# Convolution steps over GpSimd that begin five column groups later

## The chip, the cores and the metric

The kernel runs on one core of a Trainium2 chip. The metric is the device time of one execution in microseconds, the median of three runs. A core has TensorE (PE; its weight loads are PEld), VectorE (DVE), ScalarE (ACT), GpSimd (POOL) and SyncE (SP), whose queue starts all the transfers here. Each engine works off its own instructions in the order in which they were written, and waits where one needs another engine's result.

## The reference

One inference step of a small diffusion backbone: 2 layers over 1024 sample tokens and 128 prompt tokens of width 1024. In each layer three branches share one input projection, and their outputs go together into one output projection; then comes an MLP.

```python
h = _rms(x, n1) * (1 + sc1) + sh1
u_conv, qa, ka, va, qn, kn, vn = jnp.split(h @ w_in, idx, axis=-1)
a_out = _conv_module(u_conv, dw_w, dw_b, ln_g, ln_b)      # 256 channels, 31 taps over the tokens
...                                                       # b_out: grouped-query attention
...                                                       # c_out: neighbourhood attention
x = x + g1 * (jnp.concatenate([a_out, b_out, c_out], axis=-1) @ w_out)
h = _rms(x, n2) * (1 + sc2) + sh2
x = x + g2 * (jnp.square(jax.nn.relu(h @ w1)) @ w2)

def _conv_module(u, dw_w, dw_b, ln_g, ln_b):
    a, g = jnp.split(u, 2, axis=-1)
    h = a * jax.nn.sigmoid(g)
    h = lax.conv_general_dilated(h, dw_w[:, None, :], ..., feature_group_count=CONV_CH) + dw_b
    return jax.nn.silu(_layer_norm(h, ln_g, ln_b))
```

The convolution is depthwise: each channel is a sum of 31 shifted copies of itself, each times its own weight.

## The kernel before, in words

The program is written out by hand: Python generators are advanced in turn, and what each writes at its turn stands in that place on its engine. Nothing reorders it later.

**Projection** (`project`). The columns of `w_in` come in blocks: V0 and V1 (the convolution's 512 columns), then A0 to A5 and VN, 256 columns each. A0 and A1 hold the queries and keys that get the rotary positions, a good deal of GpSimd work. The seven blocks from A0 on run over five groups of token tiles each, 35 column groups in all, with 48 matmuls for a group of two tiles (tile `pst`). In each group, after the matmuls and ahead of the head norm, `project` advances the convolution by one call. While A5 and VN are written, the start of the attention is already mixed in: key building (tiles `k`, `kd`, `pstr`) and the scan of the first unit's maxima.

**Convolution.** The channels are two halves of 128, j = 0 and j = 1. `cin[j]` is the gated input, `acc[j]` (tile `cacc`) the sum, 1167 elements long. `conv_tap` writes one of the 31 steps. All of half 0, and steps 22 to 30 of half 1, are one VectorE instruction each (L102, `cacc<-cin,vecs,cacc`). Steps 0 to 21 of half 1 go another way: ScalarE makes a scaled copy (tile `cp`, L93) and GpSimd adds it (L596, `cacc<-cacc,cp`); step 0 is ScalarE's alone. `conv_taps` orders them by a counter n, which is 0 in the third of the 35 groups and goes up by one with each call. Half 0 comes first on VectorE. The nine VectorE steps of half 1 may start only when all the 22 others are written, since they add to the same `acc`; then one or two are written in a call, in turn.

After the last step `conv_all` writes the layer norm over both halves in three pieces of the tokens: sums on TensorE (tiles `psmu`, `psvr`), then `cacc<-psmu`, `lsq`, `lrs` and so on on VectorE and ScalarE, one small step to a call, 39 calls. `conv_out` then writes the result into the input of the output projection (tiles `HA`), 16 calls.

**Attention.** `gqa` has six units u = 0 to 5: three pairs of heads, and two halves of the sample tokens. A unit goes over nine key tiles, in two steps each. For each key tile TensorE makes scores (`psst`), ScalarE the exponentials (`pt`), TensorE the weighted sum (`psacc`), and the row sums R are added up: GpSimd for key tiles 1 to 6, VectorE for the last two. In the same steps runs the scan for the next unit: 24 matmuls (`psm`) and 24 maxima over them on VectorE (`mx`), then their spread over TensorE (`nmx`, `psnm`). The eight PSUM banks are shared by all of it. After the scan of unit 0 in the projection's last groups come six units, and `attention` advances the convolution by one call in every second step:

```python
        tail = conv_out(L)
        n = natten(L)
        for i, _ in enumerate(g):
            if i % 2:
                next(tail, None)
            next(fill, None)
            if L.unit == 5 and (not L.prepared or i in (6 * 18 - 5, 6 * 18 - 2)):
                next(n)
        run(tail)
```

The loop has 108 steps, so 54 calls; what is left of the convolution after it is written at once by `run(tail)`. `fill` is the modulation of the layer: a product with the `ada_w` matrix (tiles `aw`, `psmod`, `mt`, `psmt`), at whose end VectorE makes `mod` and `A`. Its weights come through the same SP queue as the projection's weights and the stores of the projected columns. After the units come the neighbourhood attention, the output projection and the MLP, which the change does not touch.

Of the kernel before, what the change touches and what calls it, by code (L numbers as in the profile page):

```python
# [45 lines left out]
def hybrid_step(ctx, tc, I, O, depth=DEPTH):  # L46
# [536 lines left out]
    def conv_tap(L, j, k):  # L583
        cin, acc = L.cin[j], L.acc[j]
        if j == 0 or k >= POOL_TAPS:
            if k == 0:
                ts(acc[:, 0:CW], cin[:, 0:CW], dww(L.l, j, 0), ALU.mult, cvec(L.l, 0, j), ALU.add)
            else:
                stt(acc[:, 0:CW], cin[:, k:k + CW], dww(L.l, j, k), acc[:, 0:CW], ALU.mult, ALU.add)
        else:  # L590
            if k == 0:
                act(acc[:, 0:CW], cin[:, 0:CW], ACTF.Identity, scale=dww(L.l, j, 0), bias=cvec(L.l, 0, j))
            else:
                p = S([CW], n="cp")
                act(p, cin[:, k:k + CW], ACTF.Copy, scale=dww(L.l, j, k))
                nc.gpsimd.tensor_tensor(out=acc[:, 0:CW], in0=acc[:, 0:CW], in1=p, op=ALU.add)  # L596

    def conv_taps(L):

        d = [(0, k) for k in range(CONV_K)] + [(1, k) for k in range(POOL_TAPS, CONV_K)]  # L600
        p = [(1, k) for k in range(POOL_TAPS)]
        n = 0
        while d or p:
            if p and n > 6:
                conv_tap(L, *p.pop(0))
            for _ in range(2 if n <= 6 else 1 + n % 2):
                if d and (d[0][0] == 0 or not p):
                    conv_tap(L, *d.pop(0))
            n += 1
            yield  # L610
# [135 lines left out]

    def conv_all(L):
        yield from conv_taps(L)
        l = L.l
        L.cin = None  # L750
# [1272 lines left out]
```

## Time and profile before

| | |
|---|---|
| median of three runs | 2948.95 us (2948.65 to 2950.8) |
| the profiled execution | 2947.94 us, of it span 2946.1 us |
| TensorE matmul busy | 2835.9 us, 96% of the span |
| VectorE, ScalarE, GpSimd busy | 2036.5, 1419.1 and 651.0 us |
| mean granted TensorE clock | 0.989 |
| projection and grouped-query units of layer 0 | some 120 to 540 us of the span |
| the same of layer 1 | some 1570 to 2000 us |

A row of the chain of waits shows a start, a length and the work that the end of the program depended on at that time. A row of the timeline shows start, length, engine, line, operation, output and input tiles and count, and in brackets how long the engine stood idle before it and what ended that. TensorE's matmuls are pipelined and their ends are modelled, so that a TensorE that is 96% busy may still have waits in it. Times are of the profiled execution, in us from the start of its span.

### The profile page before, as it was taken

Reading aid. Unit: us, or ns where it says so; the run is one execution under the profiler, and the core shown is the slowest. Engines: PE = TensorE matmul, PEld = TensorE weight load, DVE = VectorE, ACT = ScalarE, POOL = GpSimd, SP = SyncE. Lnnn points to the kernel's source line nnn. Section 1 sums busy time; section 2 is a strip of 40 time slices with the busy share of each in tenths; the row PEclk is TensorE's granted clock in tenths of the full one; section 3 lists DMA queues with packets and bytes.
Section 4 is the critical chain, followed back from the end, with each engine's and each line's share of the span. In section 5 each row is a group of like instructions: output and inputs, shape, how many; then the busy total and the mean of one; then the engine's idle time right before and its main releaser. Section 6 shows DMA issues by size and latency. Waiting matters only on the chain.

```text
span 2946.1 us, 52867 instructions
## 1 busy us (share of the span) xinstructions
PE 2835.9 (96%) x20328; PEld 2513.9 (85%) x20328; DVE 2036.5 (69%) x4007; ACT 1419.1 (48%) x2936; POOL 651.0 (22%) x597
## 2 busy tenths in 40 slices
PE   7999999999999999999989999999999999999998
PEld 4789645899999989999878885458999999999998
DVE  6576778855867756668776757778467777585766
ACT  5335366853744443433552454568446444433343
POOL 2577246310000000000236763553100000000000
PEclk9999999999999999999999999999999999999999
DMA  8377202424566678443443780033336665665334
GB/s 291 96 203 203 81 17 56 112 80 133 173 201 207 212 235 297 158 144 96 141 141 86 198 236 27 17 94 78 112 118 205 192 208 190 223 206 183 116 103 161
DMA packets 434876, 444.05 MB, mean 151 GB/s; under 512 B 120512, under 2 KB 308672, under 8 KB 434624
## 3 DMA queue, kind: packets, MB, share of 16 engines
q1 hardware_dynamic: 434624, 440.67, 48.2%
q8 instruction: 160, 2.62, 0.4%
q14 instruction: 92, 0.75, 0.1%
HBM read 307.41 MB, written 133.17 MB: 150 GB/s over the span
## 4 chain that ended last, share of the span: by engine, by line
PE 81%; DVE 8%; DMA 4%; ACT 3%; POOL 2%; issue 2%; SPq 1%; DVEq 0%; POOLq 0%; ACTq 0%
PE ps L1345 23%; PE psb L1345 8%; PE psc L1345 7%; PE pso L1345 5%; PE psa L1345 5%; PE pst L567 3%; PE pst L568 3%; PE pst L569 3%; PE psacc L1144 3%; PE psd L1345 3%; PE pspv L1011 2%; PE pspt L995 2%; PE psst L1158 2%; PE psm L1070 2%; PE psst L1159 1%
## 5 line engine op out<-in xcount | busy, mean ns | idle before, releaser
L1345 PE MATMUL ps<-ts,w2h 128*128 128x288 f32 x3072 | 535.3, 296 | 8.3 <-DVE ts L99 4.8
L1345 PEld LDWEIGHTS ps<-ts,w2h 128*128 128x128 f32 x3072 | 452.4, 189 | 9.2 <-DVE ts L99 5.3
L1345 PE MATMUL ps<-ts,w2l 128*128 128x288 f32 x1536 | 329.0, 295 | 0.0
L96 ACT CAST ts<-ti 128x576 fp32r<-128x576 f32 x256 | 172.1, 672 | 320.8 <-PE ps L1345 147.8
L567 PE MATMUL pst<-wh,HA 128*128 128x256 f32 x1040 | 295.2, 284 | 0.0
L568 PE MATMUL pst<-wl,HA 128*128 128x256 f32 x1040 | 292.0, 281 | 0.0
L569 PE MATMUL pst<-wh,HA 128*128 128x256 f32 x1040 | 291.4, 280 | 0.0
L93 ACT ACTIVATE ev<-ev 128x576 f32<-128x576 f32 x240 | 164.7, 686 | 259.5 <-DVE ev L99 255.7
L1345 PEld LDWEIGHTS ps<-ts,w2l 128*128 128x128 f32 x1536 | 247.6, 189 | 0.2
L102 DVE SCALAR_TENSOR_TENSOR X<-ps,mod,X 128x288 f32<-128x288 f32 x336 | 112.1, 409 | 176.0 <-PE ps L1345 176.0
L99 DVE TENSOR_TENSOR ts<-ti,ts 128x576 fp32r<-128x576 f32 x256 | 199.7, 780 | 32.1 <-ACT ts L96 30.5
L567 PEld LDWEIGHTS pst<-wh,HA 128*128 128x128 f32 x1040 | 195.6, 188 | 19.2 <-PE pst L569 5.2
L568 PEld LDWEIGHTS pst<-wl,HA 128*128 128x128 f32 x1040 | 195.8, 188 | 0.1
L569 PEld LDWEIGHTS pst<-wh,HA 128*128 128x128 f32 x1040 | 195.8, 188 | 0.0
L1813 POOL COPY yu<-X 128x128 f32<-128x128 f32 x8 | 4.0, 510 | 839.4 <-DVE X L102 811.1
L99 POOL TENSOR_TENSOR nacc<-nacc,nsq 128x512 f32<-128x512 f32 x3 | 3.9, 1298 | 791.2 <-PE ps L1345 791.1
L1345 PE MATMUL pso<-HA,woh 128*128 128x288 f32 x1024 | 177.6, 295 | 0.0
L1072 DVE TENSOR_REDUCE mx<-psm 128x1 f32<-128x384 f32 x288 | 142.1, 546 | 29.5 <-PE psm L1070 29.3
L93 ACT ACTIVATE pt<-psst 128x512 f32<-128x512 f32 x216 | 118.0, 597 | 87.1 <-PE psst L1159 86.0
L99 POOL TENSOR_TENSOR R<-R,pt 128x1024 f32<-128x1024 f32 x60 | 149.5, 2492 | 24.5 <-ACT pt L93 22.4
L1345 PEld LDWEIGHTS pso<-HA,woh 128*128 128x128 f32 x1024 | 149.5, 188 | 0.0
L99 DVE TENSOR_TENSOR w1l<-w1r,w1h 128x512 fp32r<-128x512 f32 x128 | 88.0, 689 | 87.0 <-ACT w1h L96 87.0
(281 smaller groups left out, 7229.4 us busy)
## 6 DMA issues: line engine op xcount, KB each, us to landing
ti<-hd SPq DMA_DIRECT2D x128, 576.0 KB, 4.0
hd<-ev SPq DMA_DIRECT2D x224, 288.0 KB, 4.1
w1r<-in_mlp_w SPq DMA_DIRECT2D x176, 256.0 KB, 4.0
aw<-in_ada_w SPq DMA_DIRECT2D x160, 256.0 KB, 4.1
HF<-in_mlp_w SPq DMA_DIRECT2D x128, 256.0 KB, 5.3
ddA<-o SPq DMA_DIRECT2D x144, 128.0 KB, 3.5
wr<-in_w_in SPq DMA_DIRECT2D x28, 512.0 KB, 4.1
sd<-ev SPq DMA_DIRECT2D x24, 576.0 KB, 2.8
```

The source lines that it names most:

```text
L93: nc.scalar.activation(out=out, in_=in_, func=func, scale=scale, bias=bias, **k)
L96: nc.scalar.copy(out, in_)
L99: (eng or nc.vector).tensor_tensor(out=out, in0=a, in1=b, op=op)
L102: nc.vector.scalar_tensor_tensor(out=out, in0=a, scalar=s, in1=b, op0=op0, op1=op1)
L567: mm(o, hi, wh, start=(k == 0), stop=False)
L568: mm(o, hi, wl, start=False, stop=False)
L569: mm(o, lo, wh, start=False, stop=(k == KT - 1))
L995: nc.tensor.transpose(ps[0:n, c], self.p[j][:, o:o + n], ident)
L1011: mm(ps[64 * j:64 * j + 64, 0:128], v[j], self.at[j, i], start=(i == 0), stop=(i == nb - 1))
L1072: nc.vector.tensor_reduce(out=mx[j][:, qt, b:b + 1], in_=ps[:, 0:384], op=ALU.max, axis=AX.X)
L1144: mm(acc[64 * j:64 * j + 64, :], v, pt[:, j, :], start=(kt == 0), stop=(kt == 8))
L1345: mm(ps[h][:, 0:HH], x, y[:, h * HH:(h + 1) * HH], start=(start and z == 0), stop=(stop and z == 2), skip_group_check=True)
```

## The change

One number is other: the counter from which `conv_taps` writes the steps of half 1 that go over GpSimd.

```diff
@@ conv_taps
         p = [(1, k) for k in range(POOL_TAPS)]
         n = 0
         while d or p:
-            if p and n > 6:
+            if p and n > 11:
                 conv_tap(L, *p.pop(0))
             for _ in range(2 if n <= 6 else 1 + n % 2):
                 if d and (d[0][0] == 0 or not p):
                     conv_tap(L, *d.pop(0))
             n += 1
             yield
```

The 22 steps were written in the calls n = 7 to 28, and are now in n = 12 to 33. The nine VectorE steps of half 1 were in n = 28 to 33 (1, 2, 1, 2, 1, 2), and are now in n = 33 to 38 (2, 1, 2, 1, 2, 1). Calls up to n = 32 are made in the projection, VN holding n = 28 to 32; from n = 33 on they are made in the units of the attention, one to a key tile. So all that follows, layer norm and output, moves five calls later too. The steps of half 0 stay. No instruction is added or removed, and both layers get the same order.

VectorE where the VN columns begin, in layer 0. `xn` is the head norm of the last A5 group, `k` and `kp` are the keys of the attention, `q` its queries, `cacc` the convolution. Before, and after:

```order
L99 TENSOR_TENSOR xn_3304<-pst_3262,y_3292 128x128
L99 TENSOR_TENSOR k_3076<-pstr_3256,k_3076 64x128
L99 TENSOR_TENSOR kp_3077<-pstr_3256,kp_3077 64x128
L102 SCALAR_TENSOR_TENSOR cacc_1092<-cin_732,vecs_100,cacc_1092 128x1167
L99 TENSOR_TENSOR k_3326<-pstr_3330,k_3326 64x512
L99 TENSOR_TENSOR k_3326<-pstr_3410,k_3326 64x512
L99 TENSOR_TENSOR k_3326<-pstr_3418,k_3326 64x128
L99 TENSOR_TENSOR kp_3327<-pstr_3418,kp_3327 64x128
L102 SCALAR_TENSOR_TENSOR cacc_1092<-cin_732,vecs_100,cacc_1092 128x1167 x2
L99 TENSOR_TENSOR q_3498<-pstr_3426,q_3431 64x512
```

```order
L99 TENSOR_TENSOR xn_3289<-pst_3247,y_3277 128x128
L99 TENSOR_TENSOR k_3061<-pstr_3241,k_3061 64x128
L99 TENSOR_TENSOR kp_3062<-pstr_3241,kp_3062 64x128
L99 TENSOR_TENSOR k_3311<-pstr_3315,k_3311 64x512
L99 TENSOR_TENSOR k_3311<-pstr_3394,k_3311 64x512
L99 TENSOR_TENSOR k_3311<-pstr_3402,k_3311 64x128
L99 TENSOR_TENSOR kp_3312<-pstr_3402,kp_3312 64x128
L99 TENSOR_TENSOR q_3483<-pstr_3410,q_3415 64x512
```

The steps of half 1 have left VectorE's VN stretch, seven of them in all.

GpSimd at the end of the projection and the begin of unit 0, in layer 0; `o` is the gained head norm that is stored, R the row sums. Before, and after:

```order
L596 TENSOR_TENSOR cacc_1092<-cacc_1092,cp_3298 128x1167
L497 TENSOR_TENSOR o_3287<-xn_3304,gains_527 128x128
L596 TENSOR_TENSOR cacc_1092<-cacc_1092,cp_3388 128x1167
L99 TENSOR_TENSOR R_3756<-pt_3757,pt_3784 128x1024
L99 TENSOR_TENSOR R_3756<-R_3756,pt_3826 128x1024
```

```order
L497 TENSOR_TENSOR o_3272<-xn_3289,gains_527 128x128
L596 TENSOR_TENSOR cacc_1092<-cacc_1092,cp_3373 128x1167
L596 TENSOR_TENSOR cacc_1092<-cacc_1092,cp_3468 128x1167
L596 TENSOR_TENSOR cacc_1092<-cacc_1092,cp_3560 128x1167
L596 TENSOR_TENSOR cacc_1092<-cacc_1092,cp_3645 128x1167
L596 TENSOR_TENSOR cacc_1092<-cacc_1092,cp_3696 128x1167
L596 TENSOR_TENSOR cacc_1092<-cacc_1092,cp_3797 128x1167
L99 TENSOR_TENSOR R_3746<-pt_3747,pt_3774 128x1024
L99 TENSOR_TENSOR R_3746<-R_3746,pt_3819 128x1024
```

Between the last stored head norm and the first R stood one add of the convolution, and now stand six; the last (`cp_3797`) is written in unit 0.

VectorE at the begin of unit 0, in layer 0; `mx` are the maxima of the next unit's scan. Before, and after:

```order
L99 TENSOR_TENSOR q_3793<-pstr_3773,q_3778 64x512
L1072 TENSOR_REDUCE mx_3799<-psm_3801 128x1
L1072 TENSOR_REDUCE mx_3799<-psm_3804 128x1
L102 SCALAR_TENSOR_TENSOR cacc_1092<-cin_732,vecs_100,cacc_1092 128x1167 x2
L99 TENSOR_TENSOR mod_101<-psmt_3809,vecs_100 128x16 x2
L102 SCALAR_TENSOR_TENSOR A_0_103<-mod_101,vecs_100 128x8 x2
L1072 TENSOR_REDUCE mx_3799<-psm_3820 128x1
L1072 TENSOR_REDUCE mx_3799<-psm_3823 128x1
L1072 TENSOR_REDUCE mx_3799<-psm_3835 128x1
L1072 TENSOR_REDUCE mx_3799<-psm_3838 128x1
L1072 TENSOR_REDUCE mx_3799<-psm_3847 128x1
```

```order
L99 TENSOR_TENSOR q_3783<-pstr_3763,q_3768 64x512
L1072 TENSOR_REDUCE mx_3789<-psm_3791 128x1
L1072 TENSOR_REDUCE mx_3789<-psm_3794 128x1
L102 SCALAR_TENSOR_TENSOR cacc_1092<-cin_732,vecs_100,cacc_1092 128x1167 x2
L99 TENSOR_TENSOR mod_101<-psmt_3802,vecs_100 128x16 x2
L102 SCALAR_TENSOR_TENSOR A_0_103<-mod_101,vecs_100 128x8 x2
L1072 TENSOR_REDUCE mx_3789<-psm_3813 128x1
L1072 TENSOR_REDUCE mx_3789<-psm_3816 128x1
L1072 TENSOR_REDUCE mx_3789<-psm_3828 128x1
L1072 TENSOR_REDUCE mx_3789<-psm_3831 128x1
L102 SCALAR_TENSOR_TENSOR cacc_1092<-cin_732,vecs_100,cacc_1092 128x1167
```

Two steps stand at the same place in both, but before they are the last two of half 1 and now the first two; after each four maxima one or two more follow, seven in all, where the layer norm of the first piece stood.

## The prediction

> **What bounds the kernel now.** I read the page's totals first, then a table of windows over the places where the moved instructions stand, then the chain of waits in one of those windows, then the single instructions.
>
> ```profile
> span 2946.1 us, 52867 instructions
> PE 2835.9 (96%) x20328; PEld 2513.9 (85%) x20328; DVE 2036.5 (69%) x4007; ACT 1419.1 (48%) x2936; POOL 651.0 (22%) x597
> ```
>
> TensorE sets the pace over the whole, but the change acts only in two short stages of each of the two layers. In the windows (columns: window, length, then busy time and count for PE, PEld, DVE, ACT, POOL, then granted clock, DMA share, GB/s) layer 0 has the VN columns of the projection, then units 0, 1, 2 and 4 of the grouped-query attention; the last row is unit 0 of layer 1. The borders are mine, a few us wide.
>
> ```profile
> 300.00:320.00 20.00, 20.00 (x163) 19.00 (x161) 16.49 (x23) 2.67 (x6) 1.55 (x1) 1.00 0.43 136
> 326.30:364.00 37.70, 30.89 (x135) 16.63 (x133) 32.70 (x51) 14.15 (x27) 15.69 (x6) 0.98 0.07 20
> 364.00:396.30 32.30, 31.80 (x133) 16.12 (x132) 21.73 (x44) 20.22 (x44) 17.29 (x10) 0.92 0.05 13
> 396.30:429.00 32.70, 29.05 (x126) 14.49 (x124) 27.50 (x43) 19.23 (x34) 15.73 (x7) 1.00 0.09 27
> 459.60:487.00 27.40, 27.12 (x125) 14.30 (x122) 22.81 (x39) 16.33 (x34) 16.18 (x8) 1.00 0.56 144
> 1782.00:1819.00 37.00, 30.32 (x129) 16.30 (x127) 30.97 (x50) 13.41 (x24) 15.77 (x6) 0.95 0.06 17
> ```
>
> In the projection (300 to 320) TensorE is busy all the time and the other engines hide. In the attention units it is not: unit 4 takes 27.4 us, the windows of unit 0 take 37.7 and 37.0 us (the end of the first scan is in them), and VectorE is busy for 32.7 and 31.0 us of them. The chain of waits in unit 0 of layer 0 (start, length, what) says where VectorE is the one waited for:
>
> ```profile
> 329.41 1.03 PE psnm L1061 x8
> ...
> 335.56 2.32 DVE cacc L102
> 337.91 1.43 DVE cacc L102
> 339.34 0.17 DVE mod L99 x2
> 339.51 2.15 DVE A L102 x2
> 341.66 0.48 DVE mx L1072
> ...
> 348.50 2.79 DVE lsq L99
> ...
> 356.27 2.48 DVE lsq L102
> 358.78 0.70 DVE lsq L102
> 359.50 0.69 DVE lrs L102
> 360.19 0.94 DVE mx L1072 x2
> 361.16 0.18 DVE nmx L1055
> 361.38 1.19 PE psnm L1061 x8
> ```
>
> From 335.56 to 342 the chain is convolution work and the modulation vector on VectorE, with the maxima of the next unit (mx) queued behind; TensorE needs those maxima done to get PSUM banks back and to end the unit (psnm). Unit 0 is the stage to price.
>
> **What the change takes out, and its worth.** The 22 steps of channel half 1 that go over GpSimd (one start on ScalarE, then 21 times a scaled copy on ScalarE and an add on GpSimd) keep their number and begin five calls later. Five leave the stretch after the rotary columns. Four enter the VN columns, which had one, and one enters unit 0. The rows of the tiles (ns: least, median, most; first and last start; the third is VectorE's step, called a tap here):
>
> ```profile
> L93 ACT ACTIVATE cp<-cin,vecs x42: 1254/1268/1281, 180.2 to 1752.9; 128x1167 f32<-128x1167 f32 x42
> L596 POOL TENSOR_TENSOR cacc<-cacc,cp x42: 2685/2712/3839, 184.4 to 1754.4; 128x1167 f32<-128x1167 f32 x42
> L102 DVE SCALAR_TENSOR_TENSOR cacc<-cin,vecs,cacc x78: 1417/1436/2727, 127.6 to 1794.7; 128x1167 f32<-128x1167 f32 x78
> ```
>
> Four of each are 10.8 us of GpSimd and 5.1 us of ScalarE. In the first 20 us of VN GpSimd was busy for 1.55 us and ScalarE for 2.67, so this hides. Where they leave, the gain could only come through a store that SP holds for GpSimd, with loads queued behind it. TensorE's waits in the projection of layer 0 are these (all of them from 115 to 326 us, the last of the first kind in order of time, and the next one after 326):
>
> ```profile
> PE psmod L223 <- DMA aw<-in_ada_w: 5.4, 6, 1.5
> PE pstr L810 <- ACT sq L93: 0.5, 1, 0.5
> 181.16 1.67 PE L223 MATMUL psmod<-aw,silc 128*2 128x512 f32 x4 [0.48 <-DMA aw<-in_ada_w]
> 329.41 1.03 PE L1061 MATMUL psnm<-ident,nmx 128*1 128x128 f32 x8 [2.31 <-DVE nmx L1055]
> ```
>
> The first moved add starts at 184.4 us, after the last wait for a load. So the relief is worth 0; at most it is the waits of other kinds, 0.5 and 2.3 us, 2.8 us a layer. DMA traffic is unchanged and the stores stand where they stood.
>
> The nine VectorE steps of half 1 wait for the last GpSimd step. Seven of them stood in VN and two in unit 0; now all nine stand in unit 0, one or two for each of its first six key tiles. What leaves VN frees nothing: TensorE was busy 20.0 of 20.0 us there.
>
> **What the change puts into unit 0.** Four terms, per layer.
>
> (1) The first call. It now issues the last GpSimd step and two VectorE steps that wait for it. The rows of ScalarE and GpSimd at that place:
>
> ```profile
> 333.08 1.12 ACT L93 ACTIVATE pt<-psst 128x512 f32<-128x512 f32 x2
> 334.28 2.35 POOL L99 TENSOR_TENSOR R<-pt,pt 128x1024 f32<-128x1024 f32 x1 [32.72 <-ACT pt L93]
> 338.03 3.52 POOL L99 TENSOR_TENSOR R<-R,pt 128x1024 f32<-128x1024 f32 x1 [1.40 <-ACT pt L93]
> ```
>
> The scaled copy follows the exponentials that end at 334.20 and ends at 335.47; the GpSimd add (2.7 us alone) ends near 338.2. VectorE, free at 335.5, waits 2.7 us, and the maxima behind it wait too. Then comes an exclusion that these rows show: the first tap ran 2.32 us because R held GpSimd until 336.63; R of 338.03 took 3.52 us and not 2.35 because the second tap ran until 339.34; and the two ops on A, of 8 columns, took 2.15 us and ended with that R. A tap that is not hindered takes 1.43. If VectorE goes first at 338.2, its taps end at 341.1, R at 343.45, A at 343.75: 2.1 later than 341.66. If R, queued behind the add, goes first (to 340.55), the taps end at 343.45, the second R then at 345.8, A at 346.05: 4.4 later. Nothing here tells which; I take the middle, +3.2.
>
> The Trainium skill, "SBUF — State Buffer", section "SBUF: two separate sides", says that a VectorE op with two SBUF inputs and a GpSimd op that reads SBUF shut each other out for a whole instruction, and do not share. The trace agrees (A, 2.15 us for 8 columns). By that rule the extra in term 2 is up to a whole R for each group of taps; by a rule without exclusion term 2 would stay at its low end.
>
> (2) Until the second psnm, seven more taps take the place of layer-norm ops that move five calls later: the two subtractions of the first row here, then 2.79, 2.48, 0.70 and 0.69 of the chain: 7.9 us. Seven taps at 1.43 are 10.0 us: +2.1 without hindrance. VectorE was already full there: in the 19.7 us from 341.66 to 361.38 stand 22 maxima besides (second row; third, the variance sum without hindrance, in unit 1).
>
> ```profile
> 345.30 1.27 DVE L102 SCALAR_TENSOR_TENSOR cacc<-psmu,cacc 128x512 f32<-128x512 f32 x2
> L1072 DVE TENSOR_REDUCE mx<-psm 128x1 f32<-128x384 f32 x120 | 59.3, 546 | 11.1 <-PE psm L1070 11.0
> 397.25 0.69 DVE L99 TENSOR_TENSOR lsq<-lsq,lsq 128x512 f32<-128x512 f32 x1 [0.69 <-ACT lsq L93]
> ```
>
> At 59.3 / 120 = 0.49 us they are 10.8 us, and with the 7.9 us VectorE is busy 18.7 of 19.7. So what is added lies on the path. The taps come in five groups, and each may find R running: 0 extra to 2.35 us. R holds GpSimd 2.35 of some 4.5 us per key tile, half the time, with half of it left on average: 0.6 a group, 2.9 for five. I take +5.0; ends +2.1 and +2.1 + 11.8 = +13.9.
>
> (3) The layer-norm ops that left unit 0 come in units 1 and later: the variance sum and the inverse root, at most 2.79 + 2.48 + 0.70 + 0.69 = 6.7 us, at least 0, since VectorE idles 10.6 of 32.3 us in unit 1. Unit 2, with such work, took 32.7 us against 27.4, so not all of it hides; but unit 2 now loses as much to unit 3 as it gets. I take +0.5.
>
> (4) The loop over the units makes 54 calls; 56 were left, now 61. So seven steps instead of two run after it, 64-column casts and subtractions:
>
> ```profile
> L96 ACT CAST HA<-cacc x16: 246/480/654, 482.3 to 1981.8; 128x512 fp32r<-128x512 f32 x8, 128x64 fp32r<-128x64 f32 x8
> ```
>
> Five more at 0.25 are 1.2 us on engines that have room; 0 to 1.2, I take +0.2.
>
> Sum: 3.2 + 5.0 + 0.5 + 0.2 = 8.9 us a layer. Layer 1 has the same order and the same unit 0 (37.0 against 37.7), so 17.8 us. The profiled execution took 2947.94 us (2946.1 and 1.84 around the span), 1.0 below the median of 2948.95: 2947.94 + 17.8 = 2965.7, against the median 2966.8. I forecast **2966 us**; its own range, all terms low (4.2 a layer, 2957) to the first call at its high end, half an R for each group and 1 us for the rest (13.4 a layer, 2976).
>
> **Rivals.** *Heavier.* Every group meets R in full: 4.4 + 13.9 = 18.3 a layer, 2985. For it: A, lsq (2.79 against 0.69) and the first tap were all caught. Against: R and taps then fill GpSimd and leave R late, which spreads them. Beside it stands the clock: TensorE waited some 2.5 us before the second psnm,
>
> ```profile
> 361.38 1.19 PE L1061 MATMUL psnm<-ident,nmx 128*1 128x128 f32 x8 [2.48 <-DVE nmx L1055]
> ```
>
> and the granted clock of unit 1 behind it is 0.92: some 2.6 us of 32.3. A longer wait in the first call can bring one more such stretch, 2.6 us. The Trainium skill, "TensorE: Matmul & The Clock Gate", section "What's actually happening", gives an idle window of about 3.4 us for the fall to half; here the slow clock came after a wait of 2.48 us.
>
> *No measurable change* (within 0.2%, about 5.9 us, which is what the measurement can tell). Terms low, 4.2, and the slow clock after unit 0 gone, since its end moves against the clock's window, -2.6: 1.6 a layer, 2952. For it: the slow stretches fall irregularly (0.98, 0.92, 1.00 in three units). Against: more waiting of TensorE should bring more of them.
>
> *Faster.* TensorE waited in unit 0 for layer-norm results of the convolution (the psmu and psvr matmuls, behind cacc and lsq). Without them in unit 0 TensorE would only need its PSUM banks, and unit 0 would fall from 32.0 us (329.41 to 361.38, psnm to psnm) to unit 4's 27.4: -4.6 a layer, 2939.8. It decides whether VectorE's work for one key tile stays below 27.4 / 9 = 3.04 us: four maxima 1.96 and one and a half taps 2.15 are 4.1, so it speaks against. That the change does nothing at all is excluded: the instructions move on four engines.
>
> **How the numbers follow.** Forecast 0.58, heavier 0.12, no change 0.18, faster 0.12. Slower is the first two, 0.70. The range 2949 to 2983 leaves out the faster case, the lower half of the unchanged one and the top of the heavier, about 0.2 together.
>
> **What would show it.** In unit 0 of both layers: VectorE's first cacc tap ends a wait on GpSimd's cacc of 2.5 us or more; nine taps with a mean above 1.5 us; the second psnm some 8 us later after the first psnm than the 32.0 us of now; unit 4 still 27 us; the VN columns unchanged in length. I am wrong if the taps stay near 1.43 us and unit 0 ends within 3 us of its length (then term 2), if VN gets shorter (then the worth of 0), or if units 1 to 3 take back what unit 0 loses.

## The result and the profile after

The changed kernel takes 2984.3 us (median of four runs, 2983.2 to 2988.9), the kernel before 2949.9 on the same chip: a ratio of 1.0123, 95% interval 1.0107 to 1.0138. It is 34 us slower. The forecast was slower, by 17, in a range that ends at 2983. The profiled execution took 2983.19 us, and its page begins:

```profile
span 2981.4 us, 52883 instructions
PE 2852.5 (96%) x20328; PEld 2520.0 (85%) x20328; DVE 2032.6 (68%) x4007; ACT 1418.9 (48%) x2936; POOL 648.0 (22%) x597
```

The work is the same; VectorE, ScalarE and GpSimd are busy no longer than before. TensorE's time grew in two parts: of the 35.3 us of span, 18.7 are more waiting, and 16.6 are matmuls, the same in number, that took longer; its mean granted clock fell from 0.989 to 0.983. Its units in layer 0, from the second psnm of one scan (at which the next unit can start) to that of the next; the last row of each goes to the row sums of unit 5. Columns as in the prediction's windows. Before:

```profile
329.40:361.40 32.00, 27.49 (x119) 14.42 (x120) 27.42 (x42) 13.16 (x24) 15.69 (x6) 1.00 0.00 1
361.40:396.10 34.70, 34.20 (x141) 17.72 (x141) 23.79 (x47) 20.84 (x45) 17.25 (x10) 0.90 0.07 19
396.10:429.50 33.40, 29.75 (x129) 14.64 (x128) 28.20 (x43) 19.62 (x34) 16.27 (x8) 1.00 0.10 31
429.50:460.30 30.80, 29.87 (x145) 16.36 (x143) 24.98 (x50) 18.85 (x44) 15.72 (x11) 1.00 0.02 6
460.30:488.00 27.70, 27.68 (x125) 14.48 (x126) 22.42 (x38) 16.88 (x34) 16.48 (x8) 1.00 0.56 143
488.00:538.50 50.50, 48.28 (x314) 30.95 (x312) 38.77 (x98) 36.42 (x94) 29.43 (x31) 1.00 0.30 72
```

After:

```profile
331.10:373.70 42.60, 32.19 (x116) 16.32 (x116) 32.66 (x45) 12.70 (x21) 18.41 (x7) 0.84 0.02 7
373.70:407.30 33.60, 30.84 (x141) 15.78 (x139) 25.57 (x47) 20.81 (x45) 15.21 (x10) 1.00 0.07 20
407.30:440.90 33.60, 30.94 (x133) 15.48 (x132) 27.93 (x42) 18.40 (x33) 17.96 (x8) 1.00 0.03 9
440.90:474.40 33.50, 32.99 (x141) 17.56 (x141) 23.43 (x47) 21.04 (x46) 16.05 (x10) 0.90 0.07 20
474.40:506.20 31.80, 28.91 (x129) 14.66 (x128) 26.92 (x42) 16.36 (x33) 18.07 (x9) 1.00 0.41 108
506.20:557.20 51.00, 49.19 (x314) 30.96 (x314) 39.28 (x101) 37.64 (x98) 27.57 (x30) 1.00 0.31 81
```

Unit 0 loses 10.6 us, units 1 to 5 together 6.3 (units 3 and 4 most). In layer 1 it is 7.5 (33.4 to 40.9) and 9.9 (177.3 to 187.2). Those are 34.3 us. The projection ahead of them adds 1.7 in layer 0, what lies between the units of the two layers takes back 2.6, and what follows the units of layer 1 adds 2.0. The chain of waits in unit 0 after the change:

```profile
337.44 1.16 ACT cp L93
...
338.73 2.69 POOL cacc L596
...
341.45 3.52 DVE cacc L102
...
344.99 3.39 DVE cacc L102
...
369.14 3.04 PE psmu L755 x4
372.18 1.60 PE psacc L1144 x4
373.78 0.96 PE psnm L1061 x8
```

The first four rows are the forecast's term 1: a scaled copy, the last GpSimd add, two taps. The psmu row was not in the forecast: the layer norm's first matmuls now stand just ahead of the psnm that starts unit 1. The end of A, where the prediction put the border between its terms 1 and 2, on VectorE's timeline before and after:

```profile
339.46 2.20 DVE L102 SCALAR_TENSOR_TENSOR A<-mod,vecs 128x8 f32<-128x8 f32 x2
```

```profile
348.50 0.25 DVE L102 SCALAR_TENSOR_TENSOR A<-mod,vecs 128x8 f32<-128x8 f32 x2
```

What TensorE waited for over all six units of layer 0 (us in total, times, longest), the top of the list before and after:

```profile
PE psnm L1061 <- DVE nmx L1055: 5.1, 3, 2.5
PE psst L1158 <- DVE mx L1072: 2.9, 1, 2.9
```

```profile
PE psst L1158 <- DVE A L102: 6.8, 1, 6.8
PE psnm L1061 <- DVE nmx L1055: 5.6, 3, 2.6
PE psst L1158 <- DVE mx L1072: 4.1, 2, 2.1
```

### The profile page after: what moved, and what is told of

It is laid out like the page before. It is cut to its first block, busy times and chain, and to the rows that moved or that the text cites. A ratio compares the mean times of both kernels' runs of the same rounds, so it can differ in the third digit from the quotient of the medians.

```text
span 2981.4 us, 52883 instructions
## 1 busy us (share of the span) xinstructions
PE 2852.5 (96%) x20328; PEld 2520.0 (85%) x20328; DVE 2032.6 (68%) x4007; ACT 1418.9 (48%) x2936; POOL 648.0 (22%) x597
## 4 chain that ended last, share of the span: by engine, by line
PE 78%; DVE 9%; DMA 4%; ACT 4%; issue 3%; POOL 2%; SPq 1%; DVEq 0%; POOLq 0%; ACTq 0%
PE ps L1345 23%; PE psb L1345 7%; PE psc L1345 6%; PE pso L1345 5%; PE psa L1345 5%; PE pst L567 3%; PE psacc L1144 3%; PE pst L568 3%; PE pst L569 3%; PE psd L1345 3%; PE pspv L1011 2%; PE pspt L995 2%; PE psst L1158 2%; PE psm L1070 2%; PE pstr L810 1%
## 5 line engine op out<-in xcount | busy, mean ns | idle before, releaser
L99 DVE TENSOR_TENSOR ts<-ti,ts 128x576 fp32r<-128x576 f32 x256 | 198.8, 777 | 33.3 <-ACT ts L96 32.1
```

Of the source, the lines that this page charges most:

```text
L99: (eng or nc.vector).tensor_tensor(out=out, in0=a, in1=b, op=op)
```

## The experiments

All times are medians, the ratio is to the kernel before on the same chip (2949 to 2951 us). "Rest of the units" is the time from unit 1's start to unit 5's row sums: 177.2 and 177.3 us (layers 0 and 1) before, 183.4 and 187.2 after. Each expectation names its theories for itself.

**Late begin, end as before.**

```diff
-            if p and n > 6:
-                conv_tap(L, *p.pop(0))
+            for _ in range(0 if n <= 11 else 2 if n <= 16 else 1):
+                if p:
+                    conv_tap(L, *p.pop(0))
```

> The GpSimd steps of half 1 begin at n = 12 as in the changed kernel, but two are written in each of the calls 12 to 16, so that the last stands at n = 28 as before; taps on VectorE, layer norm and output stand where they stood before. If the loss comes from what is late (taps in unit 0, or the layer norm in the later units): 2949 us, within 0.2% of before, and all units as long as before. If it comes from the late begin itself or from the denser GpSimd work in A3 (a rival): more than 2955 us.

2969.4 us, 1.0069 (1.0045 to 1.0094): over 2955, as the rival said. Units 1 to 4 of layer 0 are as before (34.8, 33.3, 30.8, 27.6 us) and unit 0 is 1.5 us longer; in layer 1 units 0 and 1 are 2.4 and 1.4 longer. Most of the loss lies where two steps are written in a call: the same 38.5 us of projection in layer 0, between the same two psmod products, before and here:

```profile
209.00:247.50 38.50, 38.50 (x327) 37.51 (x326) 32.56 (x46) 17.68 (x34) 31.42 (x15) 1.00 0.59 143
```

```profile
210.70:256.80 46.10, 40.70 (x325) 39.10 (x324) 42.75 (x45) 22.33 (x38) 45.40 (x18) 0.96 0.43 106
```

GpSimd is busy for 45.40 of 46.10 us and has become the bound; layer 1 loses the same 7.5. So where the end stays, the later units keep their length. That the late begin by itself is free this run can't show, since it packs the steps; the changed kernel, which does not, is 1.7 us longer ahead of the units of layer 0 and 2.6 shorter ahead of those of layer 1.

**Layer norm alone five calls late**, all taps as before (n > 6):

```diff
         yield from conv_taps(L)
+        for _ in range(5):
+            yield
```

> All the taps stand as before (GpSimd steps from n = 7), but five empty calls come between the last tap and the layer norm, so that the layer norm and the output are five calls later, as in the changed kernel. Theory A (displacement: the pieces of the layer norm that now fall into units 3 and 4 cost 6 to 10 us a layer, by themselves): 2961 to 2969 us, unit 0 shorter than before by some 2 to 4 us since the layer norm has left it, unit 4 at 31 to 34 us instead of 27.6. Theory B (the loss is the taps in unit 0, and the later units only inherit a slow clock from it): 2945 to 2951 us, unit 4 at 27.6 us.

2961.4 us, 1.0045 (1.003 to 1.0059). The units take 9.1 and 9.0 us more a layer. Unit 0 holds neither the seven taps nor any layer norm until its last key tiles, and is not shorter in layer 0 (32.9 us, first row; in layer 1 it is, by 1.5):

```profile
328.70:361.60 32.90, 30.23 (x117) 16.70 (x118) 20.87 (x37) 11.04 (x20) 15.33 (x6) 0.84 0.03 9
463.40:495.10 31.70, 28.86 (x129) 14.60 (x128) 26.90 (x42) 16.32 (x33) 18.02 (x9) 1.00 0.40 109
```

Unit 4 (second row) has gone from 27.7 to 31.7 us as in the changed kernel. A third of the loss is here without any tap moved.

**The delay caught up**: the changed kernel with five more calls of the convolution at steps 14 to 22 of the units.

```diff
-            if i % 2:
+            if i % 2 or i in (14, 16, 18, 20, 22):
```

> The changed kernel, but the convolution is advanced by five more calls, at the even steps 14 to 22 of the units (end of unit 0, begin of unit 1), so that from unit 1 on the layer norm stands where it stood before. Theory A: units 3 and 4 come back to 30.8 and 27.6 us, and what is left is unit 0, 8 to 10 us a layer, and a denser unit 1: 2966 to 2974 us. Theory B: the later units stay long (unit 4 over 31 us) and the time stays at 2980 to 2985 us.

2976.4 us, 1.0085 (1.0057 to 1.0114), between the two theories. Units 3 and 4 are back at 30.8 and 27.7 us, but unit 0 takes 44.1 and unit 1 38.0: the six units of layer 0 take 226.0 us as after the change, and those of layer 1 225.5 instead of 228.0.

**One call less** (begin at n = 11):

```diff
-            if p and n > 11:
+            if p and n > 10:
```

> The GpSimd steps begin at n = 11 instead of 12, one call earlier than in the changed kernel. The last of them then stands in the last VN group, and no VectorE instruction in unit 0 waits for GpSimd in the first call; eight taps stand in unit 0 instead of nine, and the layer norm is four calls late, not five. If the double exclusion in the first call (5.4 us a layer) is a large part of the loss: 2968 to 2974 us, a step down. If the loss goes with the number of calls (about 7 us for each): 2976 to 2979 us.

2981.9 us, 1.0108 (1.0085 to 1.0132): nearly the whole loss, differently spread, and above what either theory gave. Units 35.4, 36.8, 35.5, 34.1, 28.1, 50.8 us in layer 0, and the end of the first scan, from its first to its second psnm, takes 8.4 instead of 4.6 us.

**What in the late layer norm costs.** Among the operations of each piece that read two SBUF operands on VectorE are five plain ones: the sum of the two squares, two products with lrs and two with lsg. In the changed kernel's unit 4 two of them, of 128 columns, and GpSimd beside them (timeline):

```profile
489.69 3.68 DVE L99 TENSOR_TENSOR cacc<-cacc,lrs 128x128 f32<-128x128 f32 x2
489.58 1.27 POOL L99 TENSOR_TENSOR HA<-rt,HA 128x512 fp32r<-128x512 f32 x1 [4.51 <-ACT HA L96]
490.81 4.86 POOL L99 TENSOR_TENSOR R<-R,pt 128x1024 f32<-128x1024 f32 x2
```

They end as GpSimd's first R ends; in the kernel before the same two fell between two R and took 0.88 us together. So the five were given to GpSimd, for all pieces and for the small third piece alone, on the changed kernel:

```diff
-            tt(sqs[0], sqs[0], sqs[1], ALU.add)
+            tt(sqs[0], sqs[0], sqs[1], ALU.add, nc.gpsimd)     # small piece alone: only if m == 1
-                tt(a, a, y, ALU.mult)
+                tt(a, a, y, ALU.mult, nc.gpsimd)
-                tt(a, a, sg, ALU.mult)
+                tt(a, a, sg, ALU.mult, nc.gpsimd)
```

> The changed kernel (begin at n = 12) with five of the layer norm's operations of each piece on GpSimd instead of VectorE: the sum of the two squares (lsq<-lsq,lsq), the two cacc<-cacc,lrs and the two cacc<-cacc,lsg. All five read two operands from SBUF, and in the changed kernel they take up to 2.4 us where the same form takes 0.69 us (512 columns) or 0.2 to 0.3 us (128 columns) when GpSimd is idle. Theory L (the exclusion): each waits out an R of GpSimd, and that, not their work, is what the five calls' delay costs in the units 1 to 5 (6.3 and 9.9 us a layer). Then units 1 to 4 lose 2 to 4 us each, and the time falls from 2984 to about 2966 (2960 to 2972). Theory W (the work): only their own busy time counts, some 7.5 us of VectorE a layer of which VectorE is the path for perhaps a third: 2979 (2976 to 2982). A third way: GpSimd's R come late behind them, and the time stays or rises: 2984 to 2990.

2978.8 us, 1.0102 (1.0087 to 1.0117): a gain of some 6, not 18. The rest of the units came back as the exclusion wants it in layer 0 (177.15 us, as before) and by half in layer 1 (182.2). But unit 0 grew to 43.6 and 47.3 us (42.6 and 40.9 without the edit); there the taps meet R otherwise in layer 1, and why is left open.

> The changed kernel with those same five operations on GpSimd for the third piece of the tokens alone (128 columns), which in the changed kernel lies in unit 4 beside R: there two cacc<-cacc,lrs take 3.60 us together and one cacc<-cacc,lsg 2.16 us, all on the chain of waits. Theory L (the exclusion): unit 4 comes back from 31.8 us to 28 (27.7 to 28.8), units 0 to 3 stay, and the time is 2984 - 2 x 3.5 = 2977 (2975 to 2979). Theory W (the work): the five take about 1.2 us of VectorE unhindered, so unit 4 stays above 30.5 us and the time is 2982 or more.

2978.5 us, 1.0097 (1.0082 to 1.0112). Unit 4, the only one touched, in layer 0:

```profile
474.50:503.60 29.10, 28.43 (x128) 14.71 (x127) 23.01 (x38) 16.13 (x33) 17.44 (x12) 1.00 0.49 127
```

29.1 and in layer 1 29.2 us instead of 31.8 and 33.6; the work of five operations, about 1.2 us, was not worth that. So most of what unit 4 lost against the kernel before (27.7 us) is the exclusion; 1.4 and 1.5 us stay. Up to unit 4 this run has the order of the changed kernel, and yet its unit 0 took 44.0 and 42.4 us against 42.6 and 40.9: differences of 1.5 us in one unit are of the execution.

**The exclusion at the taps**: R of key tiles 1 and 2 of unit 0 on VectorE, in the changed kernel.

```diff
-  nc.gpsimd if kt <= GPOOL else nc.vector)
+  nc.gpsimd if (2 if u == 0 else 0) < kt <= GPOOL else nc.vector)
```

> The changed kernel with the row sums R of key tiles 1 and 2 of unit 0 on VectorE instead of GpSimd; in the changed kernel the first two taps of unit 0 (3.52 and 3.39 us) run beside just these two R. Theory L (the exclusion): the taps fall to 1.43 us each, VectorE takes on two R of 1.2 us: -4.1 + 2.4 = -1.7 us a layer, 2981 (2978 to 2983). Theory W (VectorE's work alone makes unit 0 long): VectorE has 2.4 us more a layer, 2989 (2987 to 2992).

2980.1 us, 1.0099 (1.0073 to 1.0125): not to be told from the changed kernel. The first row is the tap pair that took 6.93 us, the second a later pair, the third GpSimd beside that:

```profile
339.39 2.90 DVE L102 SCALAR_TENSOR_TENSOR cacc<-cin,vecs,cacc 128x1167 f32<-128x1167 f32 x2 [3.27 <-POOL cacc L596]
358.33 5.13 DVE L102 SCALAR_TENSOR_TENSOR cacc<-cin,vecs,cacc 128x1167 f32<-128x1167 f32 x2
352.96 12.71 POOL L99 TENSOR_TENSOR R<-R,pt 128x1024 f32<-128x1024 f32 x4 [13.60 <-DVE R L99]
```

The pair lost the 4.0 us that it had owed to R. VectorE took over two R of 1.22, and the later R, now in one row, caught a later pair (5.13 against 3.26). Unit 0 is 41.8 us in both layers, against 42.6 and 40.9.

**The slow clock**: ten spare matmuls ahead of the second psnm, where TensorE waits 2.3 us for the first scan (changed kernel).

```diff
                 ps = P("psnm")
+                if u == 0 and j == 1:
+                    for _ in range(10):
+                        mm(ps, kb[0].k1[:, 0:128], qs[u][0][0], start=True, stop=True)
```

> The changed kernel with ten spare matmuls (128x512, written over at once) ahead of the second spread of unit 0's maxima, where TensorE stands idle for 2.3 us and its granted clock then falls to 0.53 for 3 us: they keep TensorE busy in the wait and change nothing else. If the low clock after that wait costs what the scores lose by it (the chain from the spread to the last add of the convolution starts 2.7 us later than with the full clock), layer 0 loses 2 to 2.7 us of unit 0, and the time is 2980 (2978 to 2982; with layer 1 the same, if it has the low clock there too). If VectorE and GpSimd set the end of unit 0 anyway: 2984 (2983 to 2986), and the granted clock alone rises.

2983.6 us, 1.0117 (1.01 to 1.0134): no gain that can be told. The granted clock of unit 0 rises from 0.84 to 0.88, the unit falls from 42.6 to 41.2 us in layer 0, and in layer 1, where the clock had not fallen at that place, it stays (41.1). That one stretch of low clock is worth at most 1.4 us, no more than unit 0 differs between executions. It is not the cause; the other stretches of low clock in the units were not tried.

**One key tile between the last GpSimd add and the first tap** (changed kernel):

```diff
-                if d and (d[0][0] == 0 or not p):
+                if d and (d[0][0] == 0 or not p and n > 33):
```

> The changed kernel with one call left empty of taps: the nine VectorE taps begin with n = 34 instead of n = 33, so between the last add of GpSimd's half and the first tap there is a key tile, and VectorE has the next maxima before it in its queue. Theory A (the first call's wait for GpSimd is a loss of its own): the 3.2 us (layer 0) and 2.7 us (layer 1) in which VectorE stands idle go; the tap pair still meets an R (up to 4.0 us), and the layer norm is one call later, which costs 9.1/5 = 1.8 us a layer by the run with the late layer norm alone: 2984 - 2 x (3.0 - 1.8) = 2982 (2979 to 2985). Theory B (the pair's 6.9 us come from the two R written between the GpSimd add and VectorE's turn, so that a later start meets one R less): -2 x (3.0 + 2.0 - 1.8) = 2978 (2975 to 2980). If the delay of the layer norm decides: 2988 or more.

2951.5 us, 1.0003 (0.9994 to 1.0013). One empty call takes back the whole loss, which no theory of that expectation had. Unit 0 is 34.7 and 35.8 us, and the rest of the units, with the layer norm six calls late, 177.2 and 177.1. The unit's first tap and its last two, after the scan's end (nmx at 363.67):

```profile
339.63 3.54 DVE L102 SCALAR_TENSOR_TENSOR cacc<-cin,vecs,cacc 128x1167 f32<-128x1167 f32 x1 [0.20 <-POOL cacc L596]
363.75 2.89 DVE L102 SCALAR_TENSOR_TENSOR cacc<-cin,vecs,cacc 128x1167 f32<-128x1167 f32 x2
```

VectorE works through four maxima while GpSimd adds, and waits 0.20 us. The nine taps still take 18.8 us (18.0 in the changed kernel), so it is not that they meet R less; but A and the maxima now go first, TensorE's wait of 6.8 us for A is gone (its longest is 2.3), and two taps lie behind the scan.

**Layer norm alone six calls late**, the edit of five calls with `range(6)`:

> The kernel before with six instead of five empty calls between the last tap and the layer norm, all taps as before (five gave 2961.4). Theory P (the place against the end of the scan): with five calls the step of the second piece that inverts the root (lsq<-lrs 2.63 us, lsq<-psvr,lsq 0.69, lrs 0.69) stands on VectorE ahead of the last two maxima of unit 2, which TensorE's psnm waits for; with six it stands behind them. From the second psnm to the end of unit 5 layer 0 goes from 185.4 back to 177 to 179 us, unit 4 stays at 31.8, and the time is 2961.4 - 2 x 7 = 2947 (2944 to 2951). Theory D (the loss grows with the delay): 9.1 us a layer for five calls, 10.9 for six: 2965 (2962 to 2968).

2940.7 us, 0.9966 (0.9954 to 0.9977): six calls of delay are 21 us better than five, and 9 us better than none. Units 0 and 4:

```profile
327.50:357.20 29.70, 27.02 (x112) 15.13 (x112) 20.14 (x36) 10.95 (x20) 15.33 (x6) 0.89 0.03 10
451.40:481.50 30.10, 28.53 (x127) 14.72 (x128) 23.93 (x43) 16.53 (x34) 17.19 (x9) 1.00 0.42 114
```

The delay as such does not set the cost. What does is the place of a step against the end of a scan.

**Taps left where the change put them, one call more before the layer norm** (changed kernel):

```diff
         yield from conv_taps(L)
+        yield
```

> The changed kernel with one empty call between the last of the nine VectorE taps and the layer norm; taps stay where the change put them (n = 33 to 38). Theory P (the place against the end of the scan): psmu comes behind unit 1's psnm instead of ahead of it (it now takes 3.0 us of TensorE there), and the inversion of the root of the second piece comes behind unit 2's. Unit 0 falls from 42.6 to about 39 us, the time from the second psnm to the end of unit 5 from 183.4 and 187.2 to 177 to 178, and the tap pair's wait (3.2 us) and its 6.9 us stay: 2984 - 2 x (3.6 + 8) = 2961 (2957 to 2966). The difference to the run with the gap ahead of the taps (2951.5) is then the price of VectorE's wait for the last GpSimd add. Theory D (the loss grows with the delay of the layer norm): 2984 + 2 x 1.8 = 2988. Theory L alone (only the meetings with R count, wherever they fall): between, 2975 to 2986.

2962.9 us, 1.0044 (1.0028 to 1.0061), as the place wants it. Where unit 2's scan ends, the chain of waits of the changed kernel and VectorE's timeline here:

```profile
435.67 2.55 DVE lsq L102
...
438.25 0.70 DVE lsq L102
...
438.97 0.69 DVE lrs L102
439.66 0.94 DVE mx L1072 x2
...
440.85 1.17 PE psnm L1061 x8
442.02 0.73 PE psst L1158
```

```profile
429.17 1.02 DVE L1073 TENSOR_REDUCE mx<-psm 128x1 f32<-128x384 f32 x2 [1.40 <-PE psm L1071]
430.22 0.17 DVE L1056 TENSOR_REDUCE nmx<-mx 128x4 f32<-128x12 f32 x1
430.31 0.68 DVE L102 SCALAR_TENSOR_TENSOR lsq<-lrs 128x512 f32<-128x512 f32 x1
```

In the changed kernel the inversion of the root stands ahead of the last two maxima, for which psnm and so the whole next unit wait: 4 us, of which 1.9 are an R that the first of the three waits out, and then TensorE restarts at about half its clock (granted 0.56 from 440.8 to 447.6, first psst 0.73 us instead of 0.43 as behind unit 0). One call later it stands behind nmx and is hidden. The rest of the units falls to 175.8 and 175.6 us. Unit 0 stays long, 41.4 us in layer 0:

```profile
326.70:368.10 41.40, 31.44 (x112) 15.80 (x112) 33.76 (x43) 12.44 (x21) 18.08 (x7) 0.79 0.02 7
```

**The other direction**: begin two calls earlier than before.

```diff
-            if p and n > 6:
+            if p and n > 4:
```

> The kernel before with the same number changed the other way: the steps over GpSimd begin at n = 5 instead of 7, and end at n = 26; taps and layer norm come two calls earlier. If the time went with the place of the layer norm in equal steps (9.1 us a layer for five calls): 2949 - 2 x 3.6 = 2942 (2939 to 2945). If what counts is where single operations fall against R (Theory L), and the two calls more in A0 and A1 meet GpSimd's rotary work: about the same or slower, 2947 to 2956.

2955.7 us, 1.0016 (1.0007 to 1.0025). The rest of the units gains 5.7 and 4.5 us, and what is ahead of unit 0 loses 7.6 and 10.6: with the nine taps all in A5 and VN, two psmod products stand 12.4 instead of 7.3 us apart there.

**Versions that beat both.** The kernel before with the five operations on GpSimd (as above, all pieces):

> The kernel before (begin at n = 7) with the same five layer-norm operations of each piece on GpSimd as in the run on the changed kernel. In the kernel before they meet R as well: one lsq<-lsq,lsq of 2.85 us, one cacc<-cacc,lrs of 2.84 us and cacc<-cacc,lsg up to 1.71 us, against 0.69 us unhindered. Theory L (the exclusion): some 5 us of such waits a layer go, of which units 1 to 3 give back half: 2949 - 5 = 2944 (2940 to 2947). Theory W (they are off the path here, as unit 4 at 27.7 us without them shows): 2949 (2947 to 2951). Against both: GpSimd's R come late, as in unit 0 of layer 1 of that other run (47.4 us instead of 40.8): 2955 to 2960.

2938.4 us, 0.996 (0.9948 to 0.9972): units 0 and 2 shrink from 32.0 and 33.4 to 29.6 and 30.4 us. So the kernel before paid for these operations too, 12 us, more than either theory gave; their own time on VectorE and their waits for R go together here, and the run does not part them. And six empty calls with the small piece on GpSimd:

> The kernel before with six empty calls ahead of the layer norm (2940.7), and the five operations of the small third piece on GpSimd, where unit 4 is still 30.1 and 31.7 us long against 27.7 without that piece. Theory L (the exclusion): unit 4 falls to 28.0 to 28.8 as in the same edit of the changed kernel: 2940.7 - 1.7 - 3 = 2936 (2933 to 2939). If unit 4 is set by the work: 2940 to 2942.

2940.3 us, 0.9969 (0.9956 to 0.9982): unit 4 falls to 28.4 us in both layers, as the exclusion wants, but the time is that of the six calls alone, as the other theory had it. By the traces the units gain 4.6 us over both layers and the projection ahead of layer 0's units is 2.4 us longer; up to there the two programs are the same, so such differences are of the execution.

## Why the prediction was right and wrong

**Direction: right, place: in part.** The loss is in the units, but 16.2 of its 34.3 us lie behind unit 0, where the forecast had next to nothing. Nothing is gained in the projection, and VN is as long as before (between its psmod products 11.83 and 11.72 us). The forecast's first tap waits for GpSimd: 3.2 us in layer 0, 2.7 in layer 1. The nine taps have a mean of 2.0 us.

**Size: the failed step is term 3**, the layer norm in units 1 and later: +0.5 us a layer, on the ground that "unit 2 now loses as much to unit 3 as it gets", with 6.7 at most. It measured +6.3 and +9.9. The step counted VectorE's idle time in a unit as room. What decides is which instruction a step stands ahead of: behind nmx it is hidden, ahead of the last two maxima all of it is on the path, together with the R that it waits out and TensorE's slow restart. The run with one more call shows it: units 1 to 5 go from 183.4 and 187.2 to 175.8 and 175.6 us, below the kernel before. With five calls the second piece's root meets the end of unit 2's scan; with six it does not. The kernel before pays the same once, at the end of unit 0, where the prediction's chain has lsq 2.48 and 0.70 and lrs 0.69 ahead of the last two maxima; this fits that six calls fall below it. The sign in the prediction that unit 4 would still take 27 us failed (31.8 and 33.6), and the exclusion in it is shown by the small piece on GpSimd. Of the 9.9 in layer 1 some 4 go with the granted clock: its units 1, 4 and 5 are 1.4, 1.8 and 0.9 us longer than those of layer 0, at 0.95, 0.95 and 0.97 against 1.00, and with the spare matmuls, which leave these units' order as it is, the two layers took 184.3 and 183.7 us.

**Terms 1 and 2: near in sum, and term 2 by luck.** Together 8.2 forecast, 10.6 and 7.5 measured. Between the prediction's own borders, the time from the first psnm to the end of A grew by 5.4 us in layer 0 (12.25 to 17.6) and by 2.4 in layer 1, and that from there to the second psnm by 5.2 and 5.0 (19.72 to 24.96, 19.71 to 24.75). Term 1 (3.2, at most 4.4) let the pair run in one piece, before or behind an R; each of its taps waited out an R of its own, 6.93 us together, and TensorE stood for 6.8 us in one wait behind them. Term 2 (5.0) came out in size but not in its parts: the other seven taps took 11.1 us in layer 0, 1.1 over their unhindered length and not 2.9, and psmu, which the forecast did not have there, held TensorE for 3.0 us ahead of psnm. By the runs, unit 0 falls by 1.2 and 1.8 us with the call before the norm, which puts psmu behind psnm (42.6 to 41.4, 40.9 to 39.1; hardly more than executions differ), and by 6.7 and 3.3 more with the gap ahead of the taps (41.4 to 34.7, 39.1 to 35.8), which ends the wait for A and lets two taps fall behind the scan; 2.7 and 2.4 stay against the kernel before. Layer 1 gained less from the gap: without it its unit 0 was 2.3 us shorter than that of layer 0, at a clock of 0.87 against 0.79, and with it A took 4.85 us there beside the last GpSimd add and the first R (0.25 in layer 0).

**Term 4**: unit 5, counted above in the rest of the units, is 0.4 and 1.2 us longer, forecast 0.2; no run tries it alone.

**In medians**: of the 34.4 us, 21.5 go when the layer norm gets one call more (2962.9), 11.4 more when that call stands ahead of the taps instead (2951.5), and 1.6 are left.

**The rivals.** *Heavier* named nearly the measured time (2985), but by every group of taps meeting R in full, and only the first did. *No change* fell. *Faster* by unit 0 at 27.4 us fell here, and its mechanism is half alive: without the layer norm unit 0 still took 32.9 us when psmu stood ahead of psnm, and 29.7 us when it stood behind. Beside nine taps that does not show. *The clock*: the rule of the Trainium skill that the prediction named ("TensorE: Matmul & The Clock Gate", "What's actually happening") has an idle window of about 3.4 us. Here the fall came after a wait of 2.31 us, in the run with the layer norm five calls late, while the same wait of 2.31 us in the kernel before left the clock at 1.00:

```profile
328.72 1.83 PE L1063 MATMUL psnm<-ident,nmx 128*1 128x128 f32 x8 [2.31 <-DVE nmx L1057]
```

One such stretch is worth some 1.5 us: unit 3 took 33.6 us at a clock of 0.90 in the changed kernel and 32.0 at 0.95 in the run with the spare matmuls. But there are many: in the six units of layer 0 TensorE's waiting grew from 11.8 to 21.1 us, and its busy time, with as many matmuls, from 197.3 to 205.1 (the rows above). So 7.8 of 17.0 us show as slower matmuls. No run takes the low clock away and leaves the waits, so what share is the clock's own is open; in the run with six calls TensorE waits 8.9 us and is busy 196.5.

**Open**: the clock's own share of the loss, and why unit 0 of layer 1 grew with the operations on GpSimd.

## What to carry to other kernels

Where engines work down hand-written queues, the price of a delayed step is not its length against the idle time of a stage: find the last instruction of the stage that the next stage waits for, and see on which side of it the step falls. One call more or less was worth 33 of the 34 us here, so try the neighbours of a number before you explain its slope. A short operation with two SBUF operands on VectorE can cost as much as the GpSimd instruction beside it (3.68 us for two of 128 columns here). Moving such operations to GpSimd gained 12 us in the kernel before and some 6 in the changed one, and nothing beside the six empty calls.

## What the runs showed of the hardware

Where taps met R, GpSimd and VectorE took turns, instruction by instruction. In the changed kernel, two R on GpSimd (start, length) beside the two taps of the chain above:

```profile
341.37 2.35 POOL L99 TENSOR_TENSOR R<-pt,pt 128x1024 f32<-128x1024 f32 x1
343.80 3.35 POOL L99 TENSOR_TENSOR R<-R,pt 128x1024 f32<-128x1024 f32 x1
```

R until 343.72; the tap issued at 341.45 ends 344.97, 1.25 later; the second R, issued at 343.80, ends 347.15, 2.18 after that; the second tap, issued at 344.99, ends 348.38, 1.23 later. Each waited for the other's whole instruction, and the 6.93 us of the pair came again to the digit in both layers and in five other kernels. The prediction had let both taps run back to back, before or behind an R. The Trainium skill, "SBUF — State Buffer", section "SBUF: two separate sides", says that a VectorE operation with two SBUF inputs and a GpSimd operation that reads SBUF shut each other out for a whole instruction; the rows agree, down to the second R, which takes 3.35 us beside a tap and 2.35 us alone.
